# A decoder layer on one core: products with the values in turns between column halves, one addition per rotation, two loads' casts on ScalarE

## The chip, the cores and the metric

The kernel runs on one core of a Trainium2 chip. The core has a matrix engine (TensorE; PE in the profile, with its weight loads as PEld), VectorE (DVE), ScalarE (ACT), GpSimd (POOL) and SyncE (SP), which here only issues transfers. Each engine has a queue of its own that it works through in order; semaphores join the queues. The metric is the device time of one execution in microseconds (us); less is better.

## The reference

One layer on x (1 x 512 x 1024), with 256 memory tokens, all in float32:

```python
h = rmsnorm(x, norm_mix_g); proj = h @ w_in
# group A, 8 heads: an indexer picks 128 of the causal keys for each query
index = sum_h(relu(qi_h @ ki.T) * wi_h); sel = top_k(index, 128)
o_a = softmax(scores over sel * 96**-0.5) @ c_kv, then w_uv per head
# group B, 8 heads of 64: three dilated causal windows, merged by their denominators
o_b = dilated_attention(rope(q_b), rope(k_b), v_b)
x = x + concat(o_a, o_b) @ w_out
x = x + cross_attention(rmsnorm(x), rmsnorm(mem)) @ w_o_cross      # 4 heads of 256
x = x + square(relu(rmsnorm(x) @ w_up)) @ w_down                   # hidden 4096
out = rmsnorm(x, norm_final_g)
```

`rope` rotates pairs of columns: `[x1*cos - x2*sin, x2*cos + x1*sin]`.

## The kernel before

The 512 tokens are four blocks of 128. Large products are taken three times on halves of the operands: a value is split into a high part, rounded to fp32r (tiles `whi`, `h`, `ghi`), and the rest (`wlo`, `glo`); `mm3` adds high-high, high-low and low-high. Attention scores and the products with the values are plain fp32, which the trace shows as two instructions each.

Weights arrive through `load_weight`: a transfer into `wraw` (3 buffers), a cast to `whi`, a subtraction to `wlo` (6 buffers each). A letter per unit of the load says who does this, in `split_unit`: `P` and `V` cast on VectorE (line 127), `p` and `v` on ScalarE (line 129); the subtraction (line 130) is GpSimd's for `p` and `P`, VectorE's for `v` and `V`. The indexer's query load (`wb`) has `PPPP`, the cross key loads in `keys_cross` have `PPpp`; both have units of 128x1024.

`rope` (lines 288 and 296) multiplies a product in PSUM by tables of cosines and sines: two products into the destination, two into the scratch tile `rb`, and then two additions, one for each half of the pairs. It runs for the latent and indexer keys (`kk`, 8 times), the indexer's queries (`qtok`, tags `ghi2` and `ghi3`, 3 times), group B's queries and keys (`tok`, 8 heads, 8 times) and group A's queries (`tok`, 4 heads, 8 times).

`attend(b, ...)` handles query block b of one group, 8 heads, against n = 128 (b + 1) keys. A step takes `per` heads: two where b = 0, and in group B also where b = 1; else one. In a step:

- PE writes scores into a bank `sc` (2 of them); VectorE adds the bias (`m3` or the selection `sel`) and takes the maximum (line 424) into `p`; ScalarE takes the exponential with its sum (line 426); VectorE scales by the reciprocal (line 429).
- PE transposes `p` in blocks of 128 into a bank `tp` (2); VectorE or ScalarE copies the result into `pT` (2 buffers; in group A every third step uses a tile of tag `ct1` instead; group B's copies are all on ScalarE, line 439).
- PE multiplies with the values: for head h and each of the b + 1 chunks of keys, a product with 64 columns of values as weights, into the bank `pv` (one for all 8 heads of a block). An even head goes to partitions 0 to 63, an odd one to 64 to 127:

```python
for h, c in hs:
    r0 = (h % 2) * DH
    for kc in range(b + 1):
        mmul(pvv[r0:r0 + DH, h // 2, :], vtile[kc // 2][:, kc % 2, h * DH:(h + 1) * DH],
             pT[:, c.start + kc * P:c.start + (kc + 1) * P], start=kc == 0, stop=kc == b)
```

In a step of two heads, `order` pairs heads of equal parity in group B (0 and 2, then 1 and 3) and neighbours in group A (0 and 1). After the last head, `split_from` moves `pv` into `ghi` and `glo`.

The program is written as `group_b(0)`, `queries_a(0)`, `top_k(1)`, `group_b(1)`, `top_k(2)`, `queries_a(1)`, `memory()`, `group_b(2)`, `keys_a()`, `top_k(3)`, `group_b(3)`, `group_a(0..3)`, `keys_cross(0..1)`. A planner orders each engine's queue at build time, by the order of the program and its own estimate of when operands and buffers come free, so that projections and top-k work stand between the steps of attention. From the output projection on, PE's order is that of the program.

Of the kernel before, what the change touches and what calls it, by code (L numbers as in the profile page):

```python
# [11 lines left out]
F32 = mybir.dt.float32  # L12
F32R = mybir.dt.float32r
BF16 = mybir.dt.bfloat16
AF = mybir.ActivationFunctionType
ALU = mybir.AluOpType

P = 128
# [6 lines left out]
DH = 64  # L25
# [13 lines left out]
C_QN, C_QR, C_CKV, C_KR, C_QI, C_KI, C_WI, C_QB, C_KB, C_VB = (  # L39
    0, 512, 768, 896, 928, 1440, 1504, 1512, 2024, 2536)  # L40
# [24 lines left out]
def kernel(  # L65
# [7 lines left out]
    nc = tc.nc  # L73
# [8 lines left out]
    def nm(s):  # L82
        uid[0] += 1
        return f"{s}_{uid[0]}"
# [21 lines left out]
    def mmul(*a, **k):  # L106
        ins = nc.tensor.matmul(*a, **k)  # L107
        if ordered[0]:
            tc.keep_in_program_order(ins)

    def tpose(*a, **k):
        ins = nc.tensor.transpose(*a, **k)  # L112
# [19 lines left out]
    def load_weight(w, segs, k0, how, between=None):  # L132


        n = sum(c1 - c0 for c0, c1 in segs)
        nk = 4 if n <= 256 else 2
        his, los = [], []
        for u in range(KD // nk):
            raw = mtile([P, nk, n], F32, "wraw", 3)
            hi = mtile([P, nk, n], F32R, "whi", 6)  # L140
            lo = mtile([P, nk, n], F32R, "wlo", 6)
            rows = w[(k0 + nk * u) * P:(k0 + nk * u + nk) * P, :].rearrange("(k p) c -> p k c", p=P)
            o = 0
            for c0, c1 in segs:
                nc.sync.dma_start(raw[:, :, o:o + c1 - c0], rows[:, :, c0:c1])
                o += c1 - c0
            split_unit(raw, hi, lo, how[u % 4])
            if between is not None:
                between(u)
            for j in range(nk):  # L150
                his.append(hi[:, j, :])
                los.append(lo[:, j, :])
        return his, los
# [80 lines left out]
    att = p1b.enter_context(tc.tile_pool(name="att", bufs=1, side="right"))  # L234
# [6 lines left out]
    w_in0 = w_in[0]  # L241
# [31 lines left out]
    def rope(ps, heads, half, tabs, t, dst, dup=None):  # L273


        cos, sin, nsin = (tab[:, t, None, :].to_broadcast([P, heads, half]) for tab in tabs)
        r = r_mix[:, t:t + 1]
        n = heads * 2 * half
        rb = tmp.tile([P, 512], F32, name=nm("rb"), tag="rb", bufs=2)
        rbv = rb[:, :n].rearrange("p (h c f) -> p h c f", h=heads, c=2)  # L280
        if dup is None:
            ra = dst
        else:
            ra = tmp.tile([P, 512], F32, name=nm("ra"), tag="tok", bufs=2)[:, :n].rearrange(
                "p (h c f) -> p h c f", h=heads, c=2)

        def times(o, i, tab):
            nc.vector.scalar_tensor_tensor(o, i, r, tab, op0=ALU.mult, op1=ALU.mult)  # L288

        for c in range(2):  # L290
            times(ra[:, :, c, :], ps[:, :, c, :], cos)
        times(rbv[:, :, 0, :], ps[:, :, 1, :], nsin)
        times(rbv[:, :, 1, :], ps[:, :, 0, :], sin)
        if dup is None:
            for c in range(2):
                nc.vector.tensor_tensor(dst[:, :, c, :], ra[:, :, c, :], rbv[:, :, c, :], op=ALU.add)  # L296
        else:
            for c in range(dup):
                nc.vector.tensor_tensor(dst[:, :, c, :], ra.rearrange("p h c f -> p h (c f)"),
                                        rbv.rearrange("p h c f -> p h (c f)"), op=ALU.add)  # L300
# [7 lines left out]
    for t in range(NT):  # L308
# [22 lines left out]
        tp = bank_tp()  # L331
# [6 lines left out]


    qiT = mtile([P, NH, 3, P], F32R, "u1")  # L340
    wb = load_weight(w_in0, [(C_QI, C_QI + 512)], 0, "PPPP")
    for t in range(1, NT):
        ps = bank_mm()
        mm3(ps, h_tok(t), wb)
# [3 lines left out]
        tp = bank_tp().rearrange("p (j t) -> p j t", j=4)  # L348
        for j in range(4):
            tpose(tp[:, j, :], qtok[:, j * P:(j + 1) * P], ident)  # L350
        for i in range(2):
            src = tp[i * DH:(i + 1) * DH]
            dst = qiT[:, i::2, t - 1, :]
# [10 lines left out]
    for b in range(1, NT):  # L364
        n = P * (b + 1)
# [22 lines left out]
    for tag, col in (("u2a", C_QB), ("u2b", C_KB)):  # L388
        dst = mtile([P, 4, S], F32, tag)
        wt = load_weight(w_in0, [(col, col + 512)], 0, "pppp")  # L390
        for t in range(NT):
# [5 lines left out]
            tp = bank_tp().rearrange("p (j t) -> p j t", j=4)  # L397
# [9 lines left out]
    def attend(b, scores, bias_of, scale, vtile, chunk0, pv):  # L407


        n = P * (b + 1)  # L410
        pvv = pv.rearrange("p (j t) -> p j t", j=4)
        per = 2 if b == 0 or b == 1 and chunk0 else 1
        order = list(range(NH)) if chunk0 == 0 else [
            q + r + 2 * i for q in range(0, NH, 2 * per) for r in range(2) for i in range(per)]
        for g in range(NH // per):
            hs = [(h, slice(n * i, n * i + n)) for i, h in enumerate(order[per * g:per * g + per])]
            ps = bank_s()
            for h, c in hs:
                scores(ps[:, c], b, h, n)
            pr = (att.tile([P, 512], F32, name=nm("p"), tag="ct0", bufs=1) if chunk0 == 0 and g % 4 == 3 else  # L420
                  att.tile([P, 512], F32, name=nm("p"), tag="p", bufs=3))
            mx, sm, rc = (small(k, 4)[:, :per] for k in ("mx", "sm", "rc"))
            for i, (h, c) in enumerate(hs):
                nc.vector.tensor_tensor_reduce(pr[:, c], ps[:, c], bias_of(b, n), op0=ALU.add, op1=ALU.min,  # L424
                                               scale=-scale, scalar=3.0e38, accum_out=mx[:, i:i + 1])
                nc.scalar.activation(pr[:, c], pr[:, c], AF.Exp, bias=mx[:, i:i + 1], scale=-1.0, accum_out=sm[:, i:i + 1])  # L426
            nc.vector.reciprocal(rc, sm)
            for i, (h, c) in enumerate(hs):
                nc.vector.tensor_scalar(pr[:, c], pr[:, c], rc[:, i:i + 1], None, op0=ALU.mult)
            tp = bank_tp()  # L430
            m = n * per
            for c in range(0, m, P):
                tpose(tp[:, c:c + P], pr[:, c:c + P], ident)
            pT = (att.tile([P, 512], F32, name=nm("pT"), tag="ct1", bufs=1) if chunk0 == 0 and g % 3 == 2 else
                  att.tile([P, 512], F32, name=nm("pT"), tag="pT", bufs=2))
            if chunk0 == 0 and g % 3 != 1:
                nc.vector.tensor_copy(pT[:, :m], tp[:, :m])
            else:
                nc.scalar.copy(pT[:, :m], tp[:, :m])
            for h, c in hs:  # L440
                r0 = (h % 2) * DH
                for kc in range(b + 1):
                    mmul(pvv[r0:r0 + DH, h // 2, :], vtile[kc // 2][:, kc % 2, h * DH:(h + 1) * DH],
                         pT[:, c.start + kc * P:c.start + (kc + 1) * P], start=kc == 0, stop=kc == b)
        for i in range(2):
            q = chunk0 // 2 + i
            if heads_hi[q] is None:
                heads_hi[q] = mtile([P, 2, S], F32R, f"ghi{q}")
                heads_lo[q] = mtile([P, 2, S], F32R, f"glo{q}")
            bsl = slice(b * P, (b + 1) * P)  # L450
            split_from(pvv[:, 2 * i:2 * i + 2, :], heads_hi[q][:, :, bsl], heads_lo[q][:, :, bsl])
# [42 lines left out]
    sel = {0: cd}  # L494
# [44 lines left out]
    def top_k(b):  # L539
        n = P * (b + 1)  # L540
        for i in range(TOPK // 8):
            m8 = att.tile([P, 8], F32, name=nm("m8"), tag="m8", bufs=4)
            nc.vector.max(m8, acc[b])  # L543
            nc.vector.match_replace(acc[b], m8, acc[b], GONE)  # L544
        sel[b] = att.tile([P, n], F32, name=f"sel{b}")
        nc.vector.tensor_scalar(sel[b], acc[b], GONE_T, NEG, op0=ALU.is_gt, op1=ALU.mult)

    def scores_a(dst, b, h, n):
# [5 lines left out]
    def keys_cross(i):  # L554
        memT = state["memT"]
        if i == 0:
            state["kc"] = [mtile([P, KD, MEM], F32R, f"u2{c}") for c in "ab"]
        kc = state["kc"]
        wt = load_weight(w_kv[0], [(512 * i, 512 * i + 512)], 0, "PPpp")
        for m in range(4):  # L560
            ps = bank_mm()
            msl = slice(m * P, (m + 1) * P)
            mm3(ps[:, :MEM], ([a[:, msl] for a in wt[0]], [a[:, msl] for a in wt[1]]),
                ([memT[:, 0, k, :] for k in range(KD)], [memT[:, 1, k, :] for k in range(KD)]))
            split_from(ps[:, :MEM], kc[0][:, 4 * i + m, :], kc[1][:, 4 * i + m, :])
# [17 lines left out]
    memT, kc, res = state["memT"], state["kc"], state["res"]  # L583
# [108 lines left out]
    for i in range(2):  # L692
        wt = load_weight(w_q[0], [(512 * i, 512 * i + 512)], 0, "PPPP")
# [58 lines left out]
    for i in range(2):  # L752
        wt = load_weight(w_kv[0], [(D + 512 * i, D + 512 * i + 512)], 0, "ppPP")
# [75 lines left out]
    for g in range(4):  # L829
# [6 lines left out]
        for i in range(2):  # L836
            c0 = 1024 * g + 512 * i
            wt = load_weight(w_up[0], [(c0, c0 + 512)], 0, "vvvv")
# [143 lines left out]
```

## Time and profile before

| | |
|---|---|
| median of 3 runs | 827.75 us (827.49 to 827.82) |
| the profiled execution | 828.32 us, of which the span from first to last instruction is 826.5 us |
| mean granted TensorE clock | 0.993 |
| PE, PEld | 798.4 us (97%), 658.9 us (80%) |
| VectorE, ScalarE, GpSimd | 572.4 us (69%), 377.6 us (46%), 215.8 us (26%) |
| products with the values | 320 instructions, first at 148.9 us, last at 308.4 us |
| matrices moved | 94.13 MB by transfers, 114 GB/s on average |

Busy time of PE is that of matmuls with modelled ends: neighbours overlap, and a stretch in which PE is always busy need not be free of short drains. In rows of instructions the form is: start, length (of a run of them, from the first start to the last end), engine, line, operation, output tile from input tiles, partitions and columns, count. In rows of the chain it is start, length, engine, tile and line. Rows of stretches give busy time and the number of instructions for PE, PEld, VectorE, ScalarE and GpSimd, and then the granted clock, the share of the transfer engines and GB/s.

### The profile page before, as it was taken

Reading aid. Unit: us, or ns where it says so; the run is one execution under the profiler, and the core shown is the slowest. Engines: PE = TensorE matmul, PEld = TensorE weight load, DVE = VectorE, ACT = ScalarE, POOL = GpSimd, SP = SyncE. Lnnn points to the kernel's source line nnn. Section 1 sums busy time; section 2 is a strip of 40 time slices with the busy share of each in tenths; the row PEclk is TensorE's granted clock in tenths of the full one; section 3 lists DMA queues with packets and bytes.
Section 4 is the critical chain, followed back from the end, with each engine's and each line's share of the span. In section 5 each row is a group of like instructions: output and inputs, shape, how many; then the busy total and the mean of one; then the engine's idle time right before and its main releaser. Section 6 shows DMA issues by size and latency. Waiting matters only on the chain.

```text
span 826.5 us, 11175 instructions
## 1 busy us (share of the span) xinstructions
PE 798.4 (97%) x4066; PEld 658.9 (80%) x4066; DVE 572.4 (69%) x1204; ACT 377.6 (46%) x735; POOL 215.8 (26%) x164
## 2 busy tenths in 40 slices
PE   6899989999999999999999999999999999999995
PEld 5688867896688778788888888888888888888884
DVE  6885999998868544542675455768667766686664
ACT  5354323457756434221464544544544445345544
POOL 5744223130614225443620210120102010201132
PEclk9999999999999999999999999999999999999998
DMA  8442132102423022222542331497349734974492
GB/s 283 128 128 65 37 97 71 41 25 77 154 77 103 17 86 69 63 78 96 163 143 77 102 98 57 101 193 242 91 92 214 240 76 89 198 227 104 90 161 102
DMA packets 53223, 94.13 MB, mean 114 GB/s; under 512 B 5264, under 2 KB 11056, under 8 KB 53168
## 3 DMA queue, kind: packets, MB, share of 16 engines
q1 hardware_dynamic: 44464, 76.64, 29.7%
q0 software_dynamic: 8704, 16.78, 12.3%
q8 instruction: 32, 0.52, 0.3%
q14 instruction: 23, 0.19, 0.1%
HBM read 90.78 MB, written 2.10 MB: 112 GB/s over the span
## 4 chain that ended last, share of the span: by engine, by line
PE 81%; DVE 12%; DMA 3%; ACT 1%; issue 1%; POOL 1%; SPq 0%; POOLq 0%; ACTq 0%
PE mm L107 58%; PE sc L107 11%; PE tp L112 5%; PE pv L107 4%; DMA u2b<-in_w_down_dram 2%; PE tp L107 2%; DVE m L543 1%; DVE ghi L377 1%; DVE whi L127 1%; DVE tok L296 1%; DVE glo L544 1%; DVE rb L288 1%; DVE tok L288 1%; ACT whi L129 1%; DVE h L230 1%
## 5 line engine op out<-in xcount | busy, mean ns | idle before, releaser
L130 POOL TENSOR_TENSOR wlo<-wraw,whi 128x1024 fp32r<-128x1024 f32 (+2 forms) x59 | 138.2, 2356 | 200.4 <-ACT whi L129 115.1
L107 PE MATMUL mm<-whi,h 128*128 128x512 f32 (+2 forms) x536 | 165.0, 378 | 5.2 <-ACT whi L129 2.3
L107 PE MATMUL mm<-h,whi 128*128 128x512 f32 (+1 forms) x448 | 154.9, 369 | 0.0
L129 ACT CAST whi<-wraw 128x1024 fp32r<-128x1024 f32 (+3 forms) x103 | 105.7, 1028 | 94.6 <-PE mm L107 41.5
L107 PE MATMUL mm<-u,whi 128*128 128x512 f32 x320 | 124.8, 390 | 0.0
L107 PE MATMUL mm<-u,wlo 128*128 128x512 f32 x320 | 124.5, 389 | 0.0
L107 PEld LDWEIGHTS mm<-whi,h 128*128 128x128 f32 x536 | 100.5, 195 | 19.8 <-ACT whi L129 2.7
L107 PE MATMUL mm<-wlo,h 128*128 128x512 f32 (+2 forms) x280 | 104.6, 375 | 0.2 <-DVE wlo L130 0.2
L130 DVE TENSOR_TENSOR wlo<-wraw,whi 128x1024 fp32r<-128x1024 f32 (+1 forms) x64 | 81.0, 1266 | 30.6 <-ACT whi L129 30.2
L107 PEld LDWEIGHTS mm<-h,whi 128*128 128x128 f32 x448 | 81.0, 188 | 14.4 <-issue 1.0
L881 POOL DMA_DIRECT2D u2b<-in_w_down_dram x24 | 32.5, 1366 | 225.2 <-DMA wraw<-in_w_down_dram 122.0
L107 PE MATMUL mm<-whi,ghi 128*128 128x512 f32 x192 | 76.7, 399 | 0.0
L107 PE MATMUL mm<-whi,glo 128*128 128x512 f32 x192 | 75.4, 393 | 0.0
L107 PE MATMUL mm<-wlo,ghi 128*128 128x512 f32 x192 | 74.9, 390 | 0.0
L107 PEld LDWEIGHTS mm<-u,wlo 128*128 128x128 f32 x320 | 60.1, 188 | 12.6
L107 PEld LDWEIGHTS mm<-u,whi 128*128 128x128 f32 x320 | 60.1, 188 | 12.2
L107 PEld LDWEIGHTS mm<-wlo,h 128*128 128x128 f32 x280 | 54.3, 194 | 7.4 <-DVE wlo L130 0.6
L130 DVE TENSOR_TENSOR wlo<-u2b,whi 128x1024 fp32r<-128x1024 f32 x32 | 39.2, 1227 | 29.9 <-ACT whi L129 29.8
L129 ACT CAST whi<-u2b 128x1024 fp32r<-128x1024 f32 x32 | 33.6, 1052 | 47.5 <-DMA u2b<-in_w_down_dram 39.0
L426 ACT ACTIVATE p<-p,mx 128x128 f32<-128x128 f32 (+3 forms) x64 | 35.8, 560 | 27.8 <-DVE mx L424 27.1
L846 DVE SCALAR_TENSOR_TENSOR r<-mm,rT 128x512 f32<-128x512 f32 x32 | 22.0, 687 | 30.0 <-PE mm L107 22.8
L848 ACT ACTIVATE sq<-r 128x512 f32<-128x512 f32 x32 | 20.2, 632 | 48.6 <-DVE r L846 48.6
(250 smaller groups left out, 1476.2 us busy)
## 6 DMA issues: line engine op xcount, KB each, us to landing
wraw<-in_w_up_dram SPq DMA_DIRECT2D x32, 512.0 KB, 4.9
wraw<-in_w_down_dram SPq DMA_DIRECT2D x24, 512.0 KB, 5.8
u2b<-in_w_down_dram POOLq DMA_DIRECT2D x24, 512.0 KB, 7.8
wraw<-in_w_in_dram SPq DMA_DIRECT2D x16, 512.0 KB, 3.8
wraw<-in_w_kv_cross_dram SPq DMA_DIRECT2D x16, 512.0 KB, 3.9
wraw<-in_w_out_dram SPq DMA_DIRECT2D x8, 512.0 KB, 3.8
wraw<-in_w_q_cross_dram SPq DMA_DIRECT2D x8, 512.0 KB, 3.6
wraw<-in_w_o_cross_dram SPq DMA_DIRECT2D x8, 512.0 KB, 4.1
```

Source lines behind the costliest of these rows:

```text
L107: ins = nc.tensor.matmul(*a, **k)
L112: ins = nc.tensor.transpose(*a, **k)
L127: nc.vector.tensor_copy(hi, raw)
L129: nc.scalar.copy(hi, raw)
L130: (nc.gpsimd if how in "pP" else nc.vector).tensor_tensor(lo, raw, f32(hi), op=ALU.subtract)
L230: nc.vector.scalar_tensor_tensor(los[c], tps[i][:, j, :], g, f32(his[c]), op0=ALU.mult, op1=ALU.subtract)
L288: nc.vector.scalar_tensor_tensor(o, i, r, tab, op0=ALU.mult, op1=ALU.mult)
L296: nc.vector.tensor_tensor(dst[:, :, c, :], ra[:, :, c, :], rbv[:, :, c, :], op=ALU.add)
L426: nc.scalar.activation(pr[:, c], pr[:, c], AF.Exp, bias=mx[:, i:i + 1], scale=-1.0, accum_out=sm[:, i:i + 1])
L846: nc.vector.scalar_tensor_tensor(r, ps, 0.0, rows_ready[0], op0=ALU.max, op1=ALU.mult)
L848: nc.scalar.activation(sq, r, AF.Square)
L881: nc.gpsimd.dma_start(xw[:, u], src, accum_op=ALU.add)
```

## The change

- **Products with the values.** `attend` keeps a step's `pT` (in the dictionary `ready`) until a second step is done. Then, for each pair of heads 2j and 2j + 1 and each chunk of keys, it issues the even head's product and the odd head's product in turns. The first product of such a block waits for the second step's copy; the following ones are tied to the order written. `pT` has 3 buffers instead of 2. `sel` is BF16 instead of float32.
- **Rotation.** The two additions over 32 (or 16) columns per head become one over both halves.
- **Casts.** The letters of the indexer's query load become `pppp`, and those of the cross key loads too: four and, over both key loads, four casts go from VectorE to ScalarE.

```diff
@@ mmul
         ins = nc.tensor.matmul(*a, **k)
         if ordered[0]:
             tc.keep_in_program_order(ins)
+        return ins
@@ rope
         if dup is None:
-            for c in range(2):
-                nc.vector.tensor_tensor(dst[:, :, c, :], ra[:, :, c, :], rbv[:, :, c, :], op=ALU.add)
+            nc.vector.tensor_tensor(*(a.rearrange("p h c f -> p h (c f)") for a in (dst, ra, rbv)), op=ALU.add)
@@ indexer queries
-    wb = load_weight(w_in0, [(C_QI, C_QI + 512)], 0, "PPPP")
+    wb = load_weight(w_in0, [(C_QI, C_QI + 512)], 0, "pppp")
@@ attend
+        ready, last = {}, None
         for g in range(NH // per):
...
-                  att.tile([P, 512], F32, name=nm("pT"), tag="pT", bufs=2))
+                  att.tile([P, 512], F32, name=nm("pT"), tag="pT", bufs=3))
             if chunk0 == 0 and g % 3 != 1:
-                nc.vector.tensor_copy(pT[:, :m], tp[:, :m])
+                done = nc.vector.tensor_copy(pT[:, :m], tp[:, :m])
             else:
-                nc.scalar.copy(pT[:, :m], tp[:, :m])
-            for h, c in hs:
-                r0 = (h % 2) * DH
+                done = nc.scalar.copy(pT[:, :m], tp[:, :m])
+            ready.update((h, pT[:, c]) for h, c in hs)
+            if g % 2 == 0:
+                continue
+            for j in sorted(set(h // 2 for h in ready)):
                 for kc in range(b + 1):
-                    mmul(pvv[r0:r0 + DH, h // 2, :], vtile[kc // 2][:, kc % 2, h * DH:(h + 1) * DH],
-                         pT[:, c.start + kc * P:c.start + (kc + 1) * P], start=kc == 0, stop=kc == b)
+                    for i in range(2):
+                        h = 2 * j + i
+                        ins = mmul(pvv[i * DH:(i + 1) * DH, j, :], vtile[kc // 2][:, kc % 2, h * DH:(h + 1) * DH],
+                                   ready[h][:, kc * P:(kc + 1) * P], start=kc == 0, stop=kc == b)
+                        if last is None:
+                            tc.add_manual_dep(ins.ins, done.ins.name, mybir.DependencyInfo(
+                                mybir.DependencyClass.Sync, mybir.DependencyReason.DATA), reason="in turns")
+                        else:
+                            tc.add_manual_dep(ins.ins, last.ins.name, mybir.DependencyInfo(
+                                mybir.DependencyClass.NoSync, mybir.DependencyReason.DATA), reason="in turns")
+                        last = ins
+            ready, last = {}, None
@@ top_k
-        sel[b] = att.tile([P, n], F32, name=f"sel{b}")
+        sel[b] = att.tile([P, n], BF16, name=f"sel{b}")
@@ keys_cross
-        wt = load_weight(w_kv[0], [(512 * i, 512 * i + 512)], 0, "PPpp")
+        wt = load_weight(w_kv[0], [(512 * i, 512 * i + 512)], 0, "pppp")
```

## The prediction

> **What bounds the kernel now.** I read the page's table of engines first, then busy time by stretch, then the chain that ended last in the same stretches, and at the end the timeline around the products with the values (the tile `pv`).
>
> ```profile
> PE 798.4 (97%) x4066; PEld 658.9 (80%) x4066; DVE 572.4 (69%) x1204; ACT 377.6 (46%) x735; POOL 215.8 (26%) x164
> ...
> core 0: us, PE busy (x) PEld busy (x) DVE busy (x) ACT busy (x) POOL busy (x), PEclk, DMA share, GB/s
> 15.00:32.00 17.00, 12.79 (x92) 12.00 (x92) 16.50 (x51) 8.10 (x26) 15.10 (x16) 0.90 0.54 177
> 78.00:144.00 66.00, 60.94 (x292) 50.42 (x290) 65.03 (x172) 22.53 (x41) 21.05 (x10) 0.97 0.28 78
> 144.00:190.00 46.00, 45.90 (x292) 40.44 (x292) 43.45 (x154) 22.82 (x61) 11.23 (x8) 1.00 0.11 33
> 190.00:211.00 21.00, 20.89 (x117) 12.63 (x118) 17.18 (x61) 15.88 (x47) 1.75 (x1) 1.00 0.28 81
> 211.00:240.00 29.00, 29.00 (x184) 22.03 (x183) 21.89 (x66) 19.66 (x51) 13.04 (x6) 1.00 0.46 141
> 240.00:311.00 71.00, 71.00 (x487) 56.38 (x486) 45.81 (x130) 34.26 (x84) 19.46 (x9) 1.00 0.21 66
> ```
>
> PE is busy for 97% of the span, but the stretches differ. From 15 to 32 us and from 78 to 144 us VectorE is full (16.50 of 17, 65.03 of 66). From 144 to 190 us both are nearly full: 45.90 and 43.45 of 46. From 190 to 311 us PE is full and VectorE has room: 3.8 of 21, 7.1 of 29, 25.2 of 71. The chain says the same:
>
> ```profile
> by line: DVE m L543 16.5%; DVE ghi L377 14.6%; DVE tok L296 12.1%; DVE glo L544 11.0%; PE mm L107 9.7%; DVE tok L288 8.4%; DVE rb L288 7.9%; DVE ghi L544 7.2%; DVE ghi L375 5.1%; issue 3.1%; PE tp L112 1.8%; PE sc L107 1.6%; DVE ghi L378 0.
> ...
> by line: PE mm L107 35.3%; PE pv L107 28.6%; PE sc L107 20.0%; PE tp L112 16.8%
> ```
>
> The first row is the stretch 78 to 144 us, where VectorE's lines lead. The second is 211 to 240 us: all PE, and 28.6% of it products into `pv`, which the change touches.
>
> **Part 1: heads in pairs, column halves in turns.** Each product into `pv` is two instructions (fp32), 64 columns wide; even heads fill output partitions 0 to 63, odd heads 64 to 127. PE time under them, by stretch:
>
> ```profile
> 144.00:190.00 46.00, 6.36 (x48) 4.67 (x48) 1.65 (x4) 1.50 (x4) 1.00 0.11 33
> 190.00:211.00 21.00, 6.96 (x48) 5.03 (x48) 0.00 (x0) 0.37 (x1) 1.00 0.28 81
> 211.00:240.00 29.00, 8.92 (x64) 6.74 (x64) 1.68 (x4) 1.11 (x3) 1.00 0.46 141
> 240.00:311.00 71.00, 17.21 (x160) 13.11 (x160) 3.33 (x8) 2.96 (x8) 1.00 0.21 66
> ```
>
> That is 39.45 us for 320 instructions. What turns are worth, this trace shows already: group A's block b = 0 holds two heads, one even and one odd, with one product each, and these follow each other in the order that the change writes.
>
> ```profile
> 205.83 0.65 PE L107 MATMUL pv<-pT,u3a 128*64 128x128 f32 x4
> 206.32 0.38 PE L107 MATMUL pv<-pT,u3b 128*64 128x128 f32 x2
> ...
> 306.21 0.65 PE L107 MATMUL pv<-pT,vAa 128*64 128x128 f32 x4
> 306.70 0.60 PE L107 MATMUL pv<-pT,vAb 128*64 128x128 f32 x4
> ...
> 241.98 0.88 PE L107 MATMUL pv<-pT,vAa 128*64 128x128 f32 x12
> 245.58 0.44 PE L107 MATMUL pv<-pT,vAa 128*64 128x128 f32 x4
> ```
>
> One head alone: 6 instructions from 205.83 to 206.70, 0.87 us; 8 from 306.21 to 307.30, 1.09 us. In turns: 4 in 0.44 and 12 in 0.88 us, so 0.055 us for one more against 0.11 alone, and a fixed 0.22 us. By that line 8 in turns take 0.66 and 16 take 1.10 us. The new code issues, for group B, 2 blocks of 8 (b = 0), 2 of 16 (b = 1), 4 of 12 and 4 of 16; for group A, 2 of 8, 4 of 8, 4 of 12, 4 of 16. By stretch:
> - 144 to 190: 2 x 0.66 + 2 x 1.10 = 3.52, saving 2.8
> - 190 to 211: 4 x 0.88 = 3.52, saving 3.4
> - 211 to 240: 4 x 1.10 = 4.40, saving 4.5
> - 240 to 311: 6 x 0.66 + 4 x 0.88 + 4 x 1.10 = 11.88, saving 5.3
>
> Together 16.0 us of PE time. I don't take all of it. In 144 to 190 VectorE is idle for 2.55 us of 46, and its queue holds the top-k work; I take 2.0. In 190 to 211 VectorE's 17.18 and ScalarE's 15.88 us stand against the 17.6 that would be left, so each late copy shows: I take 2.5. In 211 to 240 I take 4.0, in 240 to 311, where both have room, 5.0. Sum 13.5, between 6 (half of the last two stretches' 9.8, and 1 from the earlier ones) and 16.0.
>
> On those turns the Trainium skill, "TensorE: Matmul & The Clock Gate", Part 3 (The mechanism), says the opposite: a weight load overlaps matmuls in flight only where the row group differs, and two column halves share all rows. By it the saving of turns would be near nothing and the sum 2.5 us. The 12 instructions in 0.88 us speak against it here.
>
> What the change adds there: the first product of a pair waits for the second head's copy into `pT`. Behind it on PE's queue are transposes and projections. While two heads' `pT` wait, a third buffer takes the next copy (2 become 3, in space that `sel` in BF16 gives up; group A has one more, tag `ct1`). I price that at nothing inside the sum: PE has transposes, scores and projections of other heads to do. Without that cover it is the slower rival below. A BF16 `sel` changes three writes and the bias read of 24 heads:
>
> ```profile
> L546 DVE TENSOR_SCALAR sel<-ghi 128x512 f32<-128x512 f32 x1 | 0.4, 427 | 0.0
> L546 DVE TENSOR_SCALAR sel<-ghi 128x384 f32<-128x384 f32 x1 | 0.4, 355 | 0.0
> L546 DVE TENSOR_SCALAR sel<-glo 128x256 f32<-128x256 f32 x1 | 0.3, 286 | 0.0
> ```
>
> The writes are 1.07 us in all; I price the whole at nothing, between half of that gained and as much lost.
>
> **Part 2: casts of two loads on ScalarE.** In the indexer's query load all four casts leave VectorE; three of them are on the chain as printed for 15 to 33 us:
>
> ```profile
> 21.36 1.05 DVE whi L127
> 26.64 0.60 DVE whi L127
> 28.28 1.95 DVE whi L127
> ...
> L129 ACT CAST whi<-wraw 128x1024 fp32r<-128x1024 f32 (+3 forms) x103 | 105.7, 1028 | 94.6 <-PE mm L107 41.5
> ```
>
> Those are 3.6 us of a stretch where VectorE is full. On ScalarE the four cost 4 x 1.03 us; it is busy 8.10 of 17 there, in front of evictions that VectorE's subtractions wait for. GpSimd makes the low halves either way and is busy 15.10 of 17: it becomes the next to be late. PE was busy 12.79 of 17, so it can give at most 4.2. I take 2.0, between -1 (one ScalarE cast in the way of an eviction) and 3.6. What is gained there is kept: the chain goes on as PE's work, and VectorE's full stretch then starts from PE's scores.
>
> ```profile
> 31.97 6.38 PE mm L107 x30
> ...
> 73.51 2.05 DVE glo L377
> ...
> 208.43 1.29 DVE L127 CAST whi<-wraw 128x1024 fp32r<-128x1024 f32 x2
> ```
>
> In the cross key load the two first casts of each half move, four in all, the first two of them the last row; VectorE has room there, ScalarE gets 4 x 1.03 us into stretches of which it uses 35.5 of 50. Price zero, between -1 and 1.
>
> **Part 3: one addition per rotation.** 27 rotations (8 small ones for the latent keys, 3 for the indexer, 8 for group B, 8 for group A) lose an instruction each.
>
> ```profile
> 96.48 0.67 DVE tok L296 x2
> ...
> L296 DVE TENSOR_TENSOR tok<-tok,rb 128x256 f32<-128x256 f32 x16 | 9.8, 647 | 0.0
> L906 DVE TENSOR_TENSOR xr<-xr,u 128x512 f32<-128x512 f32 x8 | 5.5, 686 | 0.0
> L296 DVE TENSOR_TENSOR tok<-tok,rb 128x64 f32<-128x64 f32 x16 | 4.0, 290 | 0.0
> ```
>
> Undisturbed, two halves stand for 0.67 us on the chain. One addition of 512 columns lasts 0.69 and, with the 0.08 us that neighbours overlap (two of 0.42 in 0.67), stands for 0.60: 0.07 us less. The mean of 0.647 comes from additions that meet GpSimd's subtraction:
>
> ```profile
> 23.29 2.44 POOL L130 TENSOR_TENSOR wlo<-wraw,whi 128x1024 fp32r<-128x1024 f32 x1
> 23.32 2.44 DVE L296 TENSOR_TENSOR kk<-kk,rb 128x16 f32<-128x16 f32 x2
> ```
>
> Here the second addition of a pair lasts as long as the subtraction. One addition less may or may not spare that. Where VectorE is on the chain lie some 8 of the rotations: 8 x 0.07 = 0.5 us; bounds 0 and 2.5 (one such meeting).
>
> **Sum.** 13.5 + 2.0 + 0.5 = 16.0 us. The profiled execution took 828.32 us (span 826.5, 1.8 outside it): 812.3. The median of the runs is 0.57 lower, 827.75: I predict 811.8. After 311 us nothing is changed. The one place where the chain leaves PE soon after is this cast of the cross query load:
>
> ```profile
> 344.23 2.90 DVE whi L127
> ```
>
> It depends on buffers that PE frees, so it moves with PE, and the gain should last to the end.
>
> **The rivals.**
> - *VectorE and ScalarE take over.* From 144 to 240 us the queue order is planned with top-k and memory work in it; if these engines keep their old pace, only their idle time is gained. For it: 43.45 of 46 and 17.18 of 21. Against: 7.1 of 29 free after that. Gain 1 + 1 + 2 from these stretches, 4 in group A, 1 from the casts: 9 us, 818.8.
> - *Turns bring nothing with two chunks or more of accumulation*, or weight loads of one half hold the other. Against: the rows of 241.98. Then the casts and rotations alone count: 2.5 us, 825.3.
> - *All of it lands:* 16.0 + 3.6 + 2.5 = 22.1, 805.7.
> - *Slower: waits on pairs.* In group B, three buffers mean that the copy of a pair's second head waits for the pair before to finish, and the next pair waits for that copy. There are 26 blocks. ScalarE does the copy behind an exponential:
>
> ```profile
> 205.06 0.46 ACT L439 COPY pT<-tp 128x384 f32<-128x384 f32 x1
> 206.67 0.72 ACT L426 ACTIVATE p<-p,mx 128x512 f32<-128x512 f32 x1 [1.15 <-DVE mx L424]
> ```
>
>   0.46 + 0.72 = 1.18 us, 26 times, is 30.7 us against 16.0 gained: with 2.5 from the rest, 828.32 - 0.57 + 30.7 - 18.5 = 839.9. It decides from 18.5 / 26 = 0.71 us a block on. Against: PE has other heads' work in reach, and the same copies cost it little so far.
>
> **How the numbers follow.** Forecast as summed, gain 12 to 20: 0.62. VectorE and ScalarE take over: 0.20. All of it: 0.08. Turns bring nothing: 0.04. Slower: 0.06. The range from 804.5 to 820.5 us holds the first three but for their tails (0.80); its ends are the full sum with 1 us beyond and the first rival with 1.7. No change means within 0.2%, 1.7 us, about what a measurement of this kernel can tell. Faster 0.92, same 0.03, slower 0.05; a mild form of the last rival is the same as before.
>
> **What would show it.** Right: PE under `pv` falls from 39.4 to about 23 us, 12 instructions in 0.9 us; the last `pv` starts about 16 us earlier than 308; no casts of line 127 on the chain before 32 us; from 340 us on, all rows shifted by the same amount. Wrong: blocks in turns at 0.11 us an instruction; new idle time of PE from 190 to 311 us behind `pT`, or ScalarE as its releaser; VectorE full to 211 us; or a planner's order in which the gain is lost again near 345 us.

## The result

The changed kernel takes 813.62 us (median of 4 runs, 813.19 to 814.07) against 827.62 us: ratio 0.9832, 95% interval 0.9814 to 0.9849. Run again beside other kernels it was 815.15 us (812.5 to 814.5 were expected) against 826.96, ratio 0.9853 (0.9827 to 0.9878). The profiled execution took 814.07 us, span 812.3. The forecast of 811.8 us was 1.8 us low and its range held the time; of its three parts, one was sized rightly, one had the wrong sign and one was too small.

The page of the changed kernel, and its rows by stretch (busy time and count of PE, PEld, VectorE, ScalarE, GpSimd, then clock, transfers):

```profile
PE 785.9 (97%) x4066; PEld 649.0 (80%) x4066; DVE 560.0 (69%) x1169; ACT 382.5 (47%) x743; POOL 215.4 (27%) x164
...
15.00:32.00 17.00, 13.12 (x87) 12.55 (x88) 12.59 (x36) 9.93 (x28) 12.00 (x14) 0.80 0.49 158
78.00:144.00 66.00, 64.49 (x318) 53.66 (x317) 64.97 (x175) 23.72 (x46) 23.93 (x11) 1.00 0.30 84
144.00:190.00 46.00, 45.18 (x290) 37.83 (x289) 43.56 (x153) 26.14 (x70) 10.94 (x8) 1.00 0.19 56
190.00:211.00 21.00, 19.84 (x123) 11.23 (x121) 16.31 (x51) 17.73 (x46) 5.62 (x3) 1.00 0.21 68
211.00:240.00 29.00, 28.96 (x231) 24.75 (x233) 18.92 (x72) 19.70 (x53) 9.09 (x4) 0.94 0.39 128
240.00:297.50 57.50, 56.64 (x419) 44.36 (x416) 42.85 (x110) 30.46 (x76) 19.56 (x9) 1.00 0.24 74
```

PE is busy for 12.5 us less in all (16.5 less under `pv`, 4.0 more elsewhere), and is now and then idle where it hardly was (0.10 and 0.11 us from 144 to 211): 0.82 us from 144 to 190, 1.16 from 190 to 211, 0.86 from 240 on. From 78 to 144 us it is the other way round: PE is idle for 1.51 us instead of 5.06. The products with the values, with the stretches moved to where the blocks of queries now end:

```profile
144.00:190.00 46.00, 3.51 (x48) 2.54 (x48) 1.68 (x4) 1.49 (x4) 1.00 0.19 56
190.00:205.00 15.00, 3.50 (x48) 2.54 (x48) 0.00 (x0) 0.00 (x0) 1.00 0.15 52
205.00:234.00 29.00, 4.38 (x64) 3.41 (x64) 1.26 (x3) 1.11 (x3) 0.94 0.38 121
234.00:297.50 63.50, 11.60 (x160) 8.47 (x160) 3.75 (x9) 3.27 (x9) 1.00 0.25 80
```

22.99 us instead of 39.45. In the summary of the tile `pv` (duration in ns: least, median, most; first and last start in us), before and after:

```profile
L107 PE MATMUL pv<-pT,vAb x48: 272/273/273, 270.3 to 308.4; 128*64 128x128 f32 x48
```

```profile
L107 PE MATMUL pv<-pT,vAb x48: 272/273/273, 263.1 to 295.0; 128*64 128x128 f32 x48
```

The last product starts 13.4 us earlier. In every kernel below the last matmul of all follows this start by 508.1 to 508.9 us, while the time from the last matmul's start to the end of the span varies from 8.2 to 11.7 us between profiled executions, with nothing changed there. So the start of the last product is the steadier measure of what a part does, and I give both. It stood at 295.0 us in the first profile of the changed kernel and at 294.8 in the second.

It is one profile for each kernel, though, and two things move it that no edit need have caused. The first is the start of the work. The first transposes that read `u2b` come before every cast and every rotation that an edit touches, and yet they start at 14.29 to 15.28 us, depending on the profile. The earliest and the latest are those of one addition alone and of the kernel before:

```profile
14.29 0.44 PE L112 MATMUL tp<-ident,u2b 128*128 128x128 f32 x2 [0.35 <-DVE h L230]
```

```profile
15.28 0.44 PE L112 MATMUL tp<-ident,u2b 128*128 128x128 f32 x2 [1.10 <-DVE h L230]
```

In the two profiles of the changed kernel they start at 15.13 and 14.93 us, and the last product follows 279.9 us later in both. So the table's last column counts from these transposes (each start taken with two places).

The second is the clock. Between 32 and 320 us most profiles hold one stretch of some 4 us with a granted clock down to 0.50. Where PE is full this takes up to 1.7 us. The changed kernel has it near 213 us, in both profiles; with the key casts back it is missing. The stretch from 200 to 225 us in these two:

```profile
200.00:225.00 25.00, 24.12 (x150) 16.78 (x147) 16.53 (x48) 22.40 (x50) 14.71 (x6) 0.93 0.40 127
```

```profile
200.00:225.00 25.00, 23.48 (x162) 16.16 (x162) 22.65 (x53) 18.18 (x45) 14.87 (x6) 1.00 0.39 127
```

It is missing, too, in pairs without turns and in one addition alone. It lies at 136 to 140 us in the kernel before, at 108 to 112 with the indexer's casts alone, at 32 to 38 with the scratch in PSUM, and between 206 and 222 in the others; with two `pT` buffers it is twice as long. Whether an edit moves it or the execution does, one profile for each kernel cannot tell. A difference of less than 2 us in the last column is therefore not safely an edit's.

### The profile page after: what moved, and what is told of

It reads as the page before. It is cut to its first block, busy times and chain, and to the rows that moved or that the text cites. A ratio compares the mean times of both kernels' runs of the same rounds, so it can differ in the third digit from the quotient of the medians.

```text
span 812.3 us, 11144 instructions
## 1 busy us (share of the span) xinstructions
PE 785.9 (97%) x4066; PEld 649.0 (80%) x4066; DVE 560.0 (69%) x1169; ACT 382.5 (47%) x743; POOL 215.4 (27%) x164
## 4 chain that ended last, share of the span: by engine, by line
PE 82%; DVE 10%; issue 3%; POOL 2%; ACT 2%; DMA 1%; SPq 0%; POOLq 0%; ACTq 0%; DVEq 0%
PE mm L107 61%; PE sc L107 11%; PE tp L113 5%; PE pv L107 3%; PE tp L107 2%; DVE glo L558 1%; DVE m L557 1%; DVE ghi L377 1%; ACT whi L130 1%; DMA u2b<-in_w_down_dram 1%; DVE whi L128 1%; DVE rb L289 1%; DVE kk L296 0%; DMA u2a<-in_x_dram 0%; DVE wlo L131 0%
## 5 line engine op out<-in xcount | busy, mean ns | idle before, releaser
L130 ACT CAST whi<-wraw 128x1024 fp32r<-128x1024 f32 (+3 forms) x111 | 114.0, 1029 | 93.9 <-PE mm L107 42.4
L107 PE MATMUL mm<-h,whi 128*128 128x512 f32 (+1 forms) x448 | 153.2, 366 | 0.0
L107 PEld LDWEIGHTS mm<-u,wlo 128*128 128x128 f32 x320 | 60.1, 188 | 12.5
L107 PEld LDWEIGHTS mm<-u,whi 128*128 128x128 f32 x320 | 60.1, 188 | 12.2
L860 DVE SCALAR_TENSOR_TENSOR r<-mm,rT 128x512 f32<-128x512 f32 x32 | 22.0, 688 | 30.3 <-PE mm L107 23.2
```

Of the source, the lines that this page charges most:

```text
L130: nc.scalar.copy(hi, raw)
L860: nc.vector.scalar_tensor_tensor(r, ps, 0.0, rows_ready[0], op0=ALU.max, op1=ALU.mult)
```

## The experiments

Each ratio is to runs of the kernel before that stood beside that kernel; their medians are 827.62, 826.65, 826.96 and 827.51 us.

| kernel | us | ratio to before, 95% interval | last product starts | counted from the first transposes |
|---|---|---|---|---|
| before | 827.62 | | 308.4 | 293.1 |
| changed | 813.62 | 0.9832, 0.9814 to 0.9849 | 295.0 | 279.9 |
| turns alone | 815.63 | 0.9870, 0.9852 to 0.9889 | 294.6 | 280.2 |
| pairs, not in turns | 818.08 | 0.9895, 0.9878 to 0.9911 | 297.2 | 282.3 |
| one addition alone | 826.55 | 0.9990, 0.9977 to 1.0002 | 305.7 | 291.4 |
| two additions again | 815.96 | 0.9870, 0.9850 to 0.9889 | 295.5 | 280.4 |
| indexer's casts alone | 829.14 | 1.0019, 1.0005 to 1.0034 | 308.5 | 294.0 |
| indexer's casts back | 811.22 | 0.9817, 0.9800 to 0.9835 | 289.6 | 274.9 |
| key casts back | 816.46 | 0.9878, 0.9846 to 0.9910 | 292.8 | 278.2 |
| all casts back | 810.57 | 0.9794, 0.9770 to 0.9817 | 290.2 | 275.0 |
| scratch in PSUM | 814.94 | 0.9866, 0.9834 to 0.9897 | 294.7 | 280.1 |
| two `pT` buffers | 816.24 | 0.9870, 0.9846 to 0.9893 | 294.6 | 280.0 |

**Turns alone.** Both letters and the two additions as before:

```diff
-    wb = load_weight(w_in0, [(C_QI, C_QI + 512)], 0, "pppp")
+    wb = load_weight(w_in0, [(C_QI, C_QI + 512)], 0, "PPPP")
...
-        wt = load_weight(w_kv[0], [(512 * i, 512 * i + 512)], 0, "pppp")
+        wt = load_weight(w_kv[0], [(512 * i, 512 * i + 512)], 0, "PPpp")
```

and in `rope` the loop over two halves. 

> Part 1 alone: pairs of heads in turns, three pT buffers and the BF16 selection, with the old letters of both loads and the old two additions. Theory (the gain of 14 us is that of the products with the values): 812 to 815 us, PE under pv about 23 us as in the changed kernel. Rival (casts and rotations gave part of the gain, or freed VectorE so that the turns could be used): 817 us or more.

815.63 us, 0.6 above what the theory allowed, and the last product at 294.6 us: as far as the whole change brings it. The other two parts together add nothing that this measure shows (280.2 and 279.9 us from the first transposes). By the time, turns alone bring 11.0 us here (9.2 to 12.2 by the interval); the whole change brought 14.0 and, run again, 11.8. PE under `pv` is 23.2 us.

**Pairs, but not in turns.**

```diff
-                for kc in range(b + 1):
-                    for i in range(2):
+                for i in range(2):
+                    for kc in range(b + 1):
                         h = 2 * j + i
```

> The changed kernel, but within a block all chunks of the even head come before all chunks of the odd head. Theory (what counts is that the two column halves alternate instruction by instruction): the blocks cost 0.11 us an instruction again, 26 blocks of 39 us less the 11 to 13 us that batching does not give; total 822 to 826 us. Rival (fewer and longer blocks, so fewer switches of the array, give the gain): 816 us or less. Second rival (weight loads of one half wait for the other, so turns never gave anything): as the changed kernel, 813 to 814 us.

818.08 us: all three fall. Blocks without turns overlap, too, in part. From the timeline of this kernel, a block of 8 and one of 12 (three chunks a head; even head 6, then odd head 6):

```profile
251.66 0.67 PE L107 MATMUL pv<-pT,vAa 128*64 128x128 f32 x8
...
198.77 0.71 PE L107 MATMUL pv<-pT,u3a 128*64 128x128 f32 x6
199.26 0.27 PE L107 MATMUL pv<-pT,u3b 128*64 128x128 f32 x1
199.32 0.27 PE L107 MATMUL pv<-pT,u3a 128*64 128x128 f32 x1
199.37 0.27 PE L107 MATMUL pv<-pT,u3b 128*64 128x128 f32 x1
199.43 0.27 PE L107 MATMUL pv<-pT,u3a 128*64 128x128 f32 x1
199.54 0.38 PE L107 MATMUL pv<-pT,u3b 128*64 128x128 f32 x2
```

and the same block of 12 in the changed kernel:

```profile
199.29 0.66 PE L107 MATMUL pv<-pT,u3a 128*64 128x128 f32 x8
199.78 0.39 PE L107 MATMUL pv<-pT,u3b 128*64 128x128 f32 x4
```

The block of 8, four instructions of one head and then four of the other, takes 0.67 us, as in turns (0.66). In the block of 12 the first row holds the even head's four `u3a` and, from 199.05 us on, the odd head's first two; the even head's last three start after that (199.15, 199.26 and 199.37). So the odd head starts when three of the even head's instructions are still to come, and runs on alone at the end. From 198.77 to 199.92 that is 1.15 us; in turns, from 199.29 to 200.17, 0.88. By the prediction's line for one head (0.22 us and 0.11 us an instruction) two separate blocks of 6 would take 1.76 us and one block of 12 without overlap 1.54: an estimate, by which fewer blocks save 0.22 us of the pair, the overlap without turns 0.39 and turns another 0.27. Under `pv` all blocks together cost, in this kernel:

```profile
144.00:300.00 156.00, 29.20 (x320) 23.16 (x320) 6.70 (x16) 5.92 (x16) 1.00 0.24 77
```

So of 16.5 us of PE time, setting the heads of a pair one behind the other saves 10.2 (fewer blocks and overlap together) and turning instruction by instruction the other 6.2. Of those 6.2 the last product shows 2.2 (297.2 to 295.0), or 2.5 counted from the first transposes. The idle time of PE, 2.9 us from 144 to 297.5 in the changed kernel and 1.4 here, and the low clock near 213 us, up to 1.7 us there and none here, would make up most of the rest.

**The indexer's casts back on VectorE.** The first diff above alone, in the changed kernel. 

> The changed kernel with the casts of the indexer's query load on VectorE again. Theory (ScalarE's casts let GpSimd's subtractions follow one another without a gap, and the addition of a small rotation on VectorE then waits through two of them, 3.9 us; the casts cost more than they save): 812 to 813.3 us, the first indexer scores near 55 instead of 56.2 us. Rival (the casts on VectorE cost what the prediction said): 815 to 816 us.

811.22 us, faster than the theory allowed, the last product 5.4 us earlier (5.0 counted from the first transposes). First scores of the indexer, in the changed kernel and here:

```profile
56.45 0.40 PE L107 MATMUL sc<-glo,u 128*128 128x256 f32 x2
```

```profile
54.50 0.40 PE L107 MATMUL sc<-glo,u 128*128 128x256 f32 x2
```

2.0 us of it are there by 56 us, 1.6 counted from the first transposes. All profiles agree on this start: the first scores come 39.7 to 39.9 us after the first transposes in the five kernels with the indexer's casts on VectorE, and 40.5 to 42.0 us after them in the eight profiles with these casts on ScalarE. The granted clock from 15 to 32 us is 0.80 in some profiles and 0.90 in others of either group, so it does not explain the step between the groups. The rest comes between 149 and 232 us, in a queue order that the planner made anew; no row shows one cause for it.

**The indexer's casts alone**, on the kernel before (`PPPP` to `pppp`, nothing else). 

> The kernel before with only the casts of the indexer's query load on ScalarE. Theory (they come later there, behind ScalarE's evictions, and the low halves with them): first indexer scores 1 to 2 us later than 55.2 us, total 828 to 831 us. Rival (the prediction's: VectorE's chain shortens by 2 us): 824.5 to 826.5 us.

829.14 us: slower by 0.19% (interval 0.05 to 0.34%), first scores 0.8 us later than 55.2, last product at the same place. Counted from the first transposes the scores are 1.5 us later and the last product 0.9. So the sign is the theory's without the rest of the change, but most of the 5.0 us needs the other parts.

**Both loads' casts back** (single addition and turns stay). 

> Turns and single additions with the old letters of both loads (all eight casts on VectorE again). Theory (each cast moved to ScalarE costs a little, the indexer's the more): last product with the values at 287 to 290 us against 295.0 in the changed kernel, total 808 to 812 us. Rival (the 5.4 us that the indexer's letters gave were the planner's luck and not the casts): last product at 292 us or later, total 813 us or more.

810.57 us and 290.2 us; the last product 0.2 us beyond the theory's window, the time inside it. This kernel and the one with the indexer's casts back are faster than the kernel before. By the last product they are ahead of the changed kernel, too, by 4.9 and 5.0 us counted from the first transposes; by the time alone this is not certain, since each one's interval overlaps one of the changed kernel's. Between the two no difference can be told.

**The key casts back**, alone. 

> The changed kernel with the first two casts of each cross key load on VectorE again. Prediction's price zero: 812.5 to 814.5 us. Rival (ScalarE is full from 190 to 211 us and the casts there delay copies): 811 to 812.5 us. Other rival (the casts on VectorE meet GpSimd's subtractions): 815 us or more.

In time not told from the changed kernel beside it (816.46 us with a wide interval, against 815.15), so the times settle none of the three. The last product is 2.2 us earlier (292.8), 1.7 counted from the first transposes: as much as the low clock can take from the changed kernel near 213 us, and this kernel has no such stretch. With the indexer's casts on VectorE, where both kernels have it, the last product comes 274.9 us after the first transposes with the key casts on ScalarE and 275.0 without. So no price of the key casts is shown.

**Two additions again**, in the changed kernel, and **one addition alone**, on the kernel before.

```diff
-            nc.vector.tensor_tensor(*(a.rearrange("p h c f -> p h (c f)") for a in (dst, ra, rbv)), op=ALU.add)
+            for c in range(2):
+                nc.vector.tensor_tensor(dst[:, :, c, :], ra[:, :, c, :], rbv[:, :, c, :], op=ALU.add)
```

> The changed kernel with two additions per rotation again. Theory (one addition saves 0.07 us a rotation on the chain from 75 to 135 us and now and then a meeting with a subtraction of GpSimd): 814 to 816.5 us. Rival (the additions lie off the path that sets the end): 813.3 to 813.9 us.

> The kernel before with only the single addition. Theory (the second addition's meetings with GpSimd's subtractions make PE idle for 3.5 us from 78 to 144 us; some of it is lost again later): PE idle there falls from 5.1 to about 1.5 us, total 824 to 826.5 us. Rival (the prediction's 0.5 us): 826.5 to 828 us.

The stretch 78 to 144 us, with two additions again and with one addition alone:

```profile
78.00:144.00 66.00, 60.85 (x299) 50.23 (x297) 65.00 (x168) 23.03 (x42) 22.38 (x11) 1.00 0.29 84
```

```profile
78.00:144.00 66.00, 64.31 (x322) 53.51 (x321) 65.00 (x183) 24.35 (x51) 20.97 (x10) 1.00 0.28 76
```

PE is idle there for 5.15 us with two and 1.69 us with one. The chain of the kernel with two additions and of the changed one shows why:

```profile
105.08 2.54 DVE tok L297 x2
...
134.04 2.48 DVE tok L297 x2
```

```profile
98.43 0.60 DVE tok L296
105.96 0.59 DVE tok L296
114.60 0.61 DVE tok L296
```

Two pairs of additions waited for a subtraction of GpSimd; none of the single ones in this stretch lasted longer than 0.85 us. At the end 2.7 us are left of it alone (308.4 to 305.7; the time's 1.0 us is not told from nothing, and 826.55 us lies where the theory and the rival meet), 0.5 in the changed kernel (815.96 us, in the theory's range), and 4.4 between turns alone and all casts back (294.6 to 290.2). Counted from the first transposes these are 1.7, 0.5 and 5.2 us. The 1.7 may be the clock alone: in the kernel before, the low clock at 136 to 140 us falls on PE's products that are the chain there (135.94 to 142.37 us), and with one addition alone it is missing.

**Scratch in PSUM.** To see whether meetings of this kind make the start late.

```diff
-        rb = tmp.tile([P, 512], F32, name=nm("rb"), tag="rb", bufs=2)
+        rb = bank("pv", 1) if heads == 1 else tmp.tile([P, 512], F32, name=nm("rb"), tag="rb", bufs=2)
```

> The changed kernel with the scratch tile rb of the eight small rotations (kk) in the bank pv, which is free at that time, so that the small addition reads one operand from PSUM. Casts of the query load stay on ScalarE. Theory (the addition waits for GpSimd's subtractions because both of its operands lie in SBUF): the addition of 3.9 us falls to 0.2 to 0.3 us, PE's row of projections starts 2 to 3 us earlier than 34.7 us, total 810 to 812 us. Rival (the start is late for another reason: ScalarE's casts or the low halves): 813 to 814.5 us with the addition short.

The changed kernel, VectorE and GpSimd at 20 us, and this one:

```profile
19.91 4.66 POOL L131 TENSOR_TENSOR wlo<-wraw,whi 128x1024 fp32r<-128x1024 f32 x2
20.59 4.03 DVE L296 TENSOR_TENSOR kk<-kk,rb 128x64 f32<-128x64 f32 x2
```

```profile
19.35 4.69 POOL L131 TENSOR_TENSOR wlo<-wraw,whi 128x1024 fp32r<-128x1024 f32 x2
19.74 0.21 DVE L296 TENSOR_TENSOR kk<-kk,pv 128x64 f32<-128x64 f32 x1
19.99 1.77 DVE L325 COPY kk<-kk 128x64 f32<-128x64 f32 x1
22.74 0.17 DVE L296 TENSOR_TENSOR kk<-kk,pv 128x32 f32<-128x32 f32 x1
```

With one operand in PSUM the additions pass while the subtractions run; the next copy within SBUF waits for 1.77 us. The mechanism is shown, and this agrees with the Trainium skill, "SBUF — State Buffer" (SBUF: two separate sides): VectorE and GpSimd share a pair of SBUF ports that one instruction holds until it ends. But PE's row of projections starts at 33.93 us instead of 34.70, which is 0.2 us earlier counted from the first transposes and not 2 to 3; the first scores come at 56.6 us, behind the low clock at 32 to 38 us, and the total does not move (814.94 us against 815.15 beside it). The meeting is not why the start is late; that part of the theory falls.

**Two `pT` buffers.** `bufs=3` to `bufs=2`. 

> The changed kernel with two pT buffers instead of three: a pair holds both, so in group B no copy can be made until the pair's products are done. Theory (waits on pairs are covered by other work on PE; with less cover they show): PE waits some 0.5 to 1 us in each of the 8 one-head pairs of group B, total 816 to 821 us. Rival (the planner fills these waits as well): 813 to 815 us.

816.24 us lies at the theory's lower edge and is not told from the changed kernel's 815.15 beside it. The last product starts at 294.6 us, no later than in the changed kernel (280.0 and 279.9 us from the first transposes), and PE is idle for 1.12 us from 190 to 211 against 1.16. So the rival holds: the third buffer is worth nothing that this shows, since work of other heads fills PE with two as well.

## Why the prediction came out as it did

By the last product, counted from the first transposes, the change breaks up in this order: turns 12.9 us (293.1 to 280.2), one addition 5.2 (to 275.0), the indexer's casts -3.2 (to 278.2), the key casts -1.7 (to 279.9). By the starts themselves these are 13.8, 4.4, -2.7 and -2.2. The third kernel of the row, with the key casts back, is the one without the low clock; with the 1.7 us that this can be worth, the indexer's casts are -4.9 and the key casts zero. In the other order the key casts are 0.1 (275.0 to 274.9) and the indexer's -5.0 (to 279.9). Forecast were 13.5, 0.5, 2.0 and zero.

The time came out near the forecast because turns are most of it. The two small parts were to bring 2.5 us together and brought about nothing: 4.7 us more than forecast for the addition, 7 less for the indexer's casts. That these misses cancel for the most part is luck.

**Turns: right.** The line of 0.22 us and 0.055 us an instruction held in every stretch: 3.52, 3.52, 4.40 and 11.88 us were forecast, 3.51, 3.50, 4.38 and 11.60 came. That 13.5 of 16.0 would last was a guess by idle time; 12.9 to 13.8 did by the last product, 11.0 by the time of turns alone, and what each stretch kept was not measured. What I gave no thought is that a good half of the PE time is had by setting the heads of a pair one behind the other. The rule that I set against the rows (loads of one column half do not overlap products of the other) does not hold here: in a block in turns the weight loads of both halves run at the same time, while the products of both run (199.29 to 199.95 us, above).

```profile
199.29 0.42 PEld L107 LDWEIGHTS pv<-pT,u3a 128*64 128x64 f32 x8 [0.17 <-issue]
```

Eight loads of 0.13 to 0.14 us each within 0.42 us.

**Casts: wrong.** The step that failed is "I take 2.0 ... What is gained there is kept". VectorE did get its time back: 12.59 us busy from 15 to 32 instead of 16.50. PE got nothing of it. Its busy time to 50 us was 7.77 + 12.79 + 18.00 = 38.56 us before and 8.44 + 13.12 + 17.02 = 38.58 after (rows 0 to 15, 15 to 32, 32 to 50), at a lower clock from 15 to 32 us (0.80 instead of 0.90) and for fewer instructions (215 before, 207 after):

```profile
0.00:15.00 15.00, 7.77 (x35) 6.45 (x35) 9.13 (x18) 7.72 (x17) 5.26 (x12) 1.00 0.83 276
...
32.00:50.00 18.00, 18.00 (x88) 14.87 (x89) 14.79 (x61) 6.96 (x18) 7.69 (x8) 1.00 0.38 108
```

```profile
0.00:15.00 15.00, 8.44 (x35) 6.82 (x35) 9.27 (x18) 7.77 (x17) 5.30 (x13) 1.00 0.86 286
...
32.00:50.00 18.00, 17.02 (x85) 13.90 (x84) 15.03 (x59) 6.73 (x19) 8.19 (x8) 1.00 0.38 114
```

And the last low half, which the scores' queries need, came later, since its cast now stood in ScalarE's queue. The kernel before, then the changed one:

```profile
28.20 2.03 DVE L127 CAST whi<-wraw 128x1024 fp32r<-128x1024 f32 x1
30.39 2.39 POOL L130 TENSOR_TENSOR wlo<-wraw,whi 128x1024 fp32r<-128x1024 f32 x1
```

```profile
30.65 1.04 ACT L130 CAST whi<-wraw 128x1024 fp32r<-128x1024 f32 x1
31.76 2.39 POOL L131 TENSOR_TENSOR wlo<-wraw,whi 128x1024 fp32r<-128x1024 f32 x1 [0.91 <-ACT whi L130]
```

It ended at 34.15 instead of 32.78 us, and the first scores came 1.3 us later. I had named this ("GpSimd ... becomes the next to be late") and left it out of the sum. That the letters make the scores late is shown by five kernels against the rest; that they do it through this later half is argued from these rows, not shown by an edit of its own.

**Rotation: too small.** The term was 8 x 0.07 us. Its bound of 2.5 us was one meeting spared; there were two. A row that I showed held the size: 16 additions with a mean of 0.647 us against 0.42 undisturbed are 3.6 us of waiting, and PE's idle time from 78 to 144 us fell by about as much, 3.4 us alone and 3.6 in the changed kernel. How much of it lasts depends on the rest: 0.5 to 5.2 us at the last product.

**Rivals.** VectorE and ScalarE took over in part only: 2.9 us of PE idle after 144 us against 0.2. The slower rival, waits on pairs, did not come about, with two buffers neither; its price was also too high as written, since the waits that it names are in group B, which has 12 of the 26 blocks. From the last product to the last matmul the distance is 508.2 us before and 508.1 after, so the gain stayed to the end, as forecast.

Open: why the indexer's casts on ScalarE cost 5 us together with the other parts and about 1 alone, why one addition is worth 5.2 us at one place and 0.5 at another, and what sets the place of the low clock. Each edit changes the planner's order of several hundred instructions, and one kernel for each order cannot part the two.

## What to carry to other kernels

Products that fill half of the array's columns, like these, should be issued next to those of the other half: side by side already overlapped them over a few instructions here, in turns over all of them, and a short stretch of the trace where this happens by chance gives the price. Time freed on an engine that is full counts only as far as the engine behind it starts earlier; check that by its idle time up to a fixed point, and follow the latest operand through the new queue. Where two engines block each other, count the meetings an edit may spare, not the length of the instruction it removes. Before a difference of 1 or 2 us between two profiles is called an edit's, compare an early instruction that no edit touches, and the granted clock.

## What the hardware showed that was not expected

- Products of two column halves do not run strictly in the order written: with three instructions of one half still to come, the other half's first product started (the block at 198.77), so that 4 + 4 instructions one after the other took 0.67 us, as long as in turns.
- Two small additions, about 0.2 us each alone, lasted through two subtractions of GpSimd (4.03 us) with both operands in SBUF; with one operand in PSUM they took 0.21 and 0.17 us at the same place.
- The granted clock fell to 0.50 for some 4 us at a time, in PE-bound stretches too, at places that differ between kernels; each time it could take up to 1.7 us.
